# Stick-breaking attention: carrying the sum over later key tiles inside the softplus terms instead of by matmuls of its own

## The chip, the cores and the metric

The kernel runs on one core of a Trainium2 chip. The metric is the device time of one execution in microseconds (us). One execution was also taken by the hardware profiler; its trace says when each instruction of each engine ran.

## What is computed

One layer of a decoder trunk: 512 tokens of width 1024. The layer has a mixer (stick-breaking attention beside a gated convolution), a cross-attention into 256 memory tokens and a gated feed-forward part. The change lies in the stick-breaking attention, 8 heads of width 64:

```python
z = jnp.einsum('bhqd,bhkd->bhqk', qb, kb) * scale
...
mask = k_pos < q_pos
log_fail = jnp.where(mask, jax.nn.log_sigmoid(-z), 0.0)
log_later = lax.cumsum(log_fail, axis=3, reverse=True) - log_fail
weights = jnp.where(mask, jnp.exp(jax.nn.log_sigmoid(z) + log_later), 0.0)
outs.append(jnp.einsum('bhqk,bhkd->bhqd', weights, vb))
```

With softplus(z) = -log_sigmoid(-z), the exponent of a weight is z minus the sum of softplus(z) over its own key and all later keys up to the query.

## The kernel before

All products are made in three passes of fp32r matmuls: each operand is split into a high part (a cast on ScalarE) and a low part (a subtraction on VectorE). The layer starts with the projection of values (to about 28 us), then comes the attention stage, then merging, memory attention, the feed-forward part and the output. TensorE's order in the attention stage is written out by hand (`manual_schedule`). ScalarE, VectorE, GpSimd and the DMA queue of SyncE are ordered there by a scheduler, from priorities, and each of them runs its instructions in that order.

The stage is a list of 16 steps, `steps`: head pair p = 0 to 3, and for each the key tiles kt = 3, 2, 1, 0 of 128 keys, the latest first. Scores are kept with keys on the 128 partitions and queries along the row; a tile kt has n = 512 - 128 kt queries. At kt=3 and kt=2 both heads of a pair share one PSUM bank (`z`, 2n columns), at kt=1 and kt=0 each head has its own. A step has three parts, which three functions emit.

- `scores` makes z = k q (L388 for kt=3 and 2, L395 on 64 partitions for kt=1 and 0), then the softplus e of z: three activations of ScalarE (L402 to L404), one operation of VectorE (L405), the causal mask on GpSimd (L355), and the split of e into the parts l (`lsplit`: L375 on ScalarE, L376 on VectorE). It also copies row 0 of z (L412, L417).
- `weights` adds to z, in PSUM, minus the running sum of softplus: `negtri` is a triangle of -1, and L438 multiplies it with the two parts of l. What the later tiles bring is added by matmuls of its own: L428 at kt=2, L434 once for each head at kt=1 and kt=0. They multiply a matrix `ones`, which holds -1 in four rows and 0 elsewhere, with the tile `rows` (named carry in the trace), which holds the carried sum of each head in a high and a low row. For the tile after, the new carried sum is row 0 of z as it was minus row 0 as it is now (L443, L448); a cast (L455) and a subtraction (L456) split it. Then come exp (L451), the mask, and the split of the weights a into ah and al (L462, L463).
- `values` multiplies the weights with v (L474), and after kt=0 the pair's output is added up and split (L482, L483, L169, L170).

TensorE's order around step i is: some halves of projections, which fill the time (L155 to L157, `fill_some`), `scores` of step i+1, `weights` of step i, `values` of step i-1. The halves bring q and k of the next pair, the convolution's inputs and some gates. Their weights are loaded by SyncE (`wr`, 512 KB each), cast (`wh`, L150) and subtracted (`wl`, L151). SyncE also moves the second half of the queries into `lq` (L300) and loads the memory tokens `mk` (L490). The latter are squared on ScalarE (L497) and summed on GpSimd (L500, L502).

Of the kernel before, what the change touches and what calls it, by code (L numbers as in the profile page):

```python
# [26 lines left out]
HS = S // 2  # L27
# [13 lines left out]
def hybrid_layer(ctx: ExitStack, tc: tile.TileContext, xT_d, memT_d, cols_d, wv_d, win_d,  # L41
                 wbr_d, wmix_d, wmq_d, wmk_d, wmv_d, wmo_d, wfi_d, wfo_d, out):
    nc = tc.nc
# [10 lines left out]
    lpool = stick.enter_context(tc.tile_pool(name="lpool", bufs=4))  # L54
# [153 lines left out]
    first = nc.scalar.dma_start(gcol, cols_d)  # L208
# [130 lines left out]

    oT = []  # L340
    steps = [(p, kt) for p in range(TT) for kt in range(TT - 1, -1, -1)]
    zs, sp, av, ops = {}, {}, {}, {}

    def span(kt):
        return kt * P, S - kt * P

    def by_head(t, kt):

        n = span(kt)[1]
        if 2 * n <= 512:  # L350
            return [t[0].rearrange("p (h n) -> p h n", n=n)]
        return [u[:, None, :] for u in t]

    def causal(t):
        nc.gpsimd.affine_select(out=t[:, :, :P], in_=t[:, :, :P], compare_op=ALU.is_gt, fill=0.0,  # L355
                                base=0, pattern=[[0, t.shape[1]], [1, P]], channel_multiplier=-1)

    rows = [lpool.tile([P, n], F32R, tag=f"carry{n}", name=f"carry{n}", bufs=1) for n in (S, HS)]  # L360
    raw_rows = [lpool.tile([P, S], F32, tag=f"row{i}", name=f"row{i}", bufs=1) for i in range(2)]
    for t in rows:
        nc.gpsimd.memset(f(t), 0.0)
    ones_f = tmp("ones", P)
    nc.gpsimd.memset(ones_f, 0.0)
    for i in range(0, P, HD // 2):
        nc.gpsimd.memset(ones_f[i:i + 1, :], -1.0)
    ones = lpool.tile([P, P], F32R, tag="ones", name="ones", bufs=1)
    nc.vector.tensor_copy(ones, ones_f)
    first = {}  # L370

    def lsplit(t, n, tag):
        hi, lo = (lpool.tile([P, n], F32R, tag=tag, name=nm(tag), bufs=4,
                             padded_shape=[P, S if tag == "l0" else S - P]) for _ in range(2))
        nc.scalar.copy(hi, t)  # L375
        nc.vector.tensor_tensor(out=lo, in0=t, in1=f(hi), op=ALU.subtract)  # L376
        return hi, lo

    def scores(p, kt):
        c0, n = span(kt)  # L380
        q, k = qk[p]
        ks = slice(kt * P, (kt + 1) * P)
        terms = (0, 0), (0, 1), (1, 0)
        if 2 * n <= 512:
            zs[p, kt] = [ztile("z")[:, :2 * n]]
            z3 = by_head(zs[p, kt], kt)[0]
            for i, (a, b) in enumerate(terms):
                nc.tensor.matmul(z3, k[a][:, ks], late_q[p % 2][b][:, :, c0 - HS:],  # L388
                                 start=i == 0, stop=i == 2)
        else:  # L390
            zs[p, kt] = [ztile("z")[:, :n] for _ in range(2)]
            for i, (a, b) in enumerate(terms):
                for h in range(2):
                    hs = slice(h * HD, (h + 1) * HD)
                    nc.tensor.matmul(zs[p, kt][h], k[a][hs, ks], q[b][hs, c0:],  # L395
                                     start=i == 0, stop=i == 2)
        sp[p, kt] = []
        with tc.high_priority(100):
            for h, z in enumerate(zs[p, kt]):
                w = z.shape[1]  # L400
                e = tmp("e")[:, :w]
                nc.scalar.activation(e, z, AF.Abs)  # L402
                nc.scalar.activation(e, e, AF.Exp, scale=-1.0)
                nc.scalar.activation(e, e, AF.Ln, bias=1.0)  # L404
                nc.vector.scalar_tensor_tensor(out=e, in0=z, scalar=0.0, in1=e, op0=ALU.max,  # L405
                                               op1=ALU.add)
                causal(by_head([e], kt)[0])
                sp[p, kt].append(lsplit(e, w, f"l{kt % 2}"))

                if kt == TT - 1:  # L410
                    first[p, kt] = [raw_rows[kt % 2][0:1, :w]]
                    nc.scalar.copy(first[p, kt][0], z[0:1, :])  # L412
                elif kt > 0:
                    for i in range(2) if w == 2 * n else (h,):
                        r = raw_rows[kt % 2][i * HD:i * HD + 1, :n]
                        first.setdefault((p, kt), []).append(r)
                        nc.scalar.copy(r, head_of(p, kt, i)[0:1, :])  # L417

    def head_of(p, kt, h):
        n = span(kt)[1]  # L420
        z = zs[p, kt]
        return z[0][:, h * n:(h + 1) * n] if len(z) == 1 else z[h]

    def weights(p, kt):
        c0, n = span(kt)
        av[p, kt] = []
        if kt == TT - 2:
            nc.tensor.matmul(by_head(zs[p, kt], kt)[0][:, :, P:], ones,  # L428
                             rows[1].rearrange("p (h n) -> p h n", h=2), start=False, stop=False,
                             skip_group_check=True)  # L430
        elif kt < TT - 2:
            for h in range(2):
                hs = slice(h * HD, (h + 1) * HD)
                nc.tensor.matmul(zs[p, kt][h][:, P:], ones[hs, :], rows[0][hs, :n - P],  # L434
                                 start=False, stop=False, skip_group_check=True)
        for z, parts in zip(zs[p, kt], sp[p, kt]):
            for part in parts:
                nc.tensor.matmul(z, negtri, part, start=False, stop=True, skip_group_check=True)  # L438
        exp_a = []
        got = first.get((p, kt), [])  # L440
        with tc.high_priority(150):
            if kt == TT - 1:
                nc.vector.tensor_tensor(out=got[0], in0=got[0], in1=zs[p, kt][0][0:1, :],  # L443
                                        op=ALU.subtract)
            for h, z in enumerate(zs[p, kt]):
                if 0 < kt < TT - 1:
                    for i in range(2) if len(zs[p, kt]) == 1 else (h,):
                        nc.vector.tensor_tensor(out=got[i], in0=got[i],  # L448
                                                in1=head_of(p, kt, i)[0:1, :], op=ALU.subtract)
                exp_a.append(tmp("a")[:, :z.shape[1]])  # L450
                exps.append(nc.scalar.activation(exp_a[h], z, AF.Exp))  # L451
            for h, r in enumerate(got):
                i = h * HD
                c = rows[1 if kt == TT - 1 else 0][:, :r.shape[1]]
                nc.scalar.copy(c[i:i + 1, :], r)  # L455
                nc.vector.tensor_tensor(out=c[i + HD // 2:i + HD // 2 + 1, :], in0=r,  # L456
                                        in1=f(c[i:i + 1, :]), op=ALU.subtract)
        for a in exp_a:
            causal(by_head([a], kt)[0])
            w = a.shape[1]  # L460
            ah, al = unit("ah")[:, :w], unit("al")[:, :w]
            nc.vector.tensor_copy(ah, a)  # L462
            nc.vector.tensor_tensor(out=al, in0=a, in1=f(ah), op=ALU.subtract)  # L463
            for i in range(w // n):
                av[p, kt].append((ah[:, i * n:(i + 1) * n], al[:, i * n:(i + 1) * n]))
# [490 lines left out]
    hs = HS  # L956
# [147 lines left out]
```

## Time and profile before

| | us |
|---|---|
| median of 3 runs (864.08 to 864.14) | 864.14 |
| the profiled execution | 864.6 |
| its span, first to last instruction | 861.8 |

| stretch of the span | TensorE busy | VectorE busy | ScalarE busy |
|---|---|---|---|
| 28 to 49 us | 21.00 of 21 | 13.83 | 11.47 |
| 49 to 202 us (16 steps of attention) | 152.66 of 153 | 132.12 | 110.11 |
| 202 to 862 us | 654.00 of 660 | 416.56 | 299.57 |

The engines are called PE (TensorE matmuls), PEld (its loads of weights), DVE (VectorE), ACT (ScalarE), POOL (GpSimd) and SP (SyncE) in the rows. In a timeline's row stand the start, the duration, the engine, the line, the operation, the tiles written and read, and their shapes; in brackets the idle time before it and what ended it. Matmuls overlap, and their ends are modelled: how long one holds TensorE is read from its start to the start of the next. In a row of a group stand the count, the busy time, the mean of one in ns, and the idle time before.

### The profile page before, as it was taken

How to read it: one execution, taken by the hardware profiler on the slowest of the kernel's cores; microseconds unless marked ns; L12 is line 12 of the kernel's file. 1: busy time of each engine (PE TensorE's matmuls, PEld its weight loads, DVE VectorE, ACT ScalarE, POOL GpSimd, SP SyncE). 2: the span in 40 equal slices, each digit the busy share in tenths (PEclk: the TensorE clock that was granted, in tenths of full speed). 3: DMA queues.
4: the chain of work that ended last, by engine and by line, in shares of the span. 5: the costliest groups of instructions: out<-in, count | busy, mean ns of one | idle time of the engine just before them, and what ended most of it. 6: DMA issues, size and time to landing. Idle time of an engine off the chain costs nothing.

```text
span 861.8 us, 12717 instructions
## 1 busy us (share of the span) xinstructions
PE 854.1 (99%) x4932; PEld 750.9 (87%) x4932; DVE 586.9 (68%) x964; ACT 440.2 (51%) x774; POOL 69.2 (8%) x105
## 2 busy tenths in 40 slices
PE   9999999999999999999999999999999999999997
PEld 7887888888888898888888889999999999888897
DVE  8768898986555466555555879888887778533334
ACT  7476787675333244443444656555445556322335
POOL 2022131111000000000000101111111100000002
PEclk9999999999999999999999999999999999999999
DMA  8432331228333345422111427777677763322202
GB/s 294 131 101 86 106 115 50 74 84 266 115 110 110 98 159 188 154 97 93 57 49 49 135 50 199 188 182 178 175 190 192 188 151 122 123 98 98 74 1 97
DMA packets 42347, 108.32 MB, mean 126 GB/s; under 512 B 4144, under 2 KB 8240, under 8 KB 42288
## 3 DMA queue, kind: packets, MB, share of 16 engines
q1 hardware_dynamic: 36016, 95.70, 32.8%
q0 software_dynamic: 5984, 11.54, 8.2%
q8 instruction: 38, 0.62, 0.3%
q10 hardware_dynamic: 288, 0.29, 0.1%
q14 instruction: 21, 0.17, 0.1%
HBM read 104.36 MB, written 2.10 MB: 124 GB/s over the span
## 4 chain that ended last, share of the span: by engine, by line
PE 98%; DVE 1%; ACT 0%; issue 0%; POOL 0%; DVEq 0%; POOLq 0%
PE z L811 15%; PE y L811 7%; PE pr L155 7%; PE pr L157 7%; PE pr L156 7%; PE f L157 5%; PE f L155 5%; PE f L156 5%; PE v L811 4%; PE r L155 3%; PE r L156 3%; PE r L157 3%; PE v L261 3%; PE mq L155 2%; PE mq L157 2%; PE mq L156 2%
## 5 line engine op out<-in xcount | busy, mean ns | idle before, releaser
L150 ACT CAST wh<-wr 128x1024 fp32r<-128x1024 f32 x106 | 111.0, 1051 | 215.2 <-issue 98.6
L151 DVE TENSOR_TENSOR wl<-wr,wh 128x1024 fp32r<-128x1024 f32 x106 | 129.4, 1223 | 100.0 <-ACT wh L150 100.0
L155 PE MATMUL pr<-xgh,wh 128*128 128x512 f32 x288 | 112.5, 391 | 0.0
L156 PE MATMUL pr<-xgl,wh 128*128 128x512 f32 x288 | 112.2, 390 | 0.0
L157 PE MATMUL pr<-xgh,wl 128*128 128x512 f32 x288 | 112.2, 390 | 0.0
L156 PE MATMUL f<-actl,wh 128*128 128x512 f32 (+1 forms) x208 | 74.2, 357 | 0.0
L155 PE MATMUL f<-acth,wh 128*128 128x512 f32 (+1 forms) x208 | 74.2, 357 | 0.0
L157 PE MATMUL f<-acth,wl 128*128 128x512 f32 (+1 forms) x208 | 74.0, 356 | 0.0
L811 PE MATMUL z<-xdh,wf 128*128 128x256 f32 x352 | 70.3, 283 | 0.0
L768 POOL DMA_DIRECT2D ws<-in_w_ffn_in_dram x22 | 26.6, 1208 | 468.7 <-DVE c L626 267.3
L157 PEld LDWEIGHTS pr<-xgh,wl 128*128 128x128 f32 x288 | 54.1, 188 | 11.4
L156 PEld LDWEIGHTS pr<-xgl,wh 128*128 128x128 f32 x288 | 54.1, 188 | 10.8
L155 PEld LDWEIGHTS pr<-xgh,wh 128*128 128x128 f32 x288 | 54.1, 188 | 10.8
L811 PEld LDWEIGHTS z<-xdh,wf 128*128 128x128 f32 x352 | 58.0, 192 | 0.0
L831 ACT COPY sa<-z 128x256 f32<-128x256 f32 x44 | 16.4, 373 | 77.8 <-PE z L811 77.8
L811 PE MATMUL z<-xdl,wf 128*128 128x256 f32 x176 | 49.8, 283 | 0.0
L802 DVE TENSOR_TENSOR wf<-s,wf 128x512 fp32r<-128x512 f32 x44 | 30.3, 690 | 20.9 <-ACT wf L801 19.8
L155 PEld LDWEIGHTS f<-acth,wh 128*128 128x128 f32 x208 | 39.3, 189 | 5.7
L157 PEld LDWEIGHTS f<-acth,wl 128*128 128x128 f32 x208 | 39.3, 189 | 5.6
L156 PEld LDWEIGHTS f<-actl,wh 128*128 128x128 f32 x208 | 39.3, 189 | 5.6
L811 PE MATMUL y<-xch,wf 128*128 128x256 f32 x176 | 35.5, 283 | 0.0
L811 PE MATMUL v<-xoh,wf 128*128 128x256 f32 x176 | 35.5, 283 | 0.0
(290 smaller groups left out, 2158.9 us busy)
## 6 DMA issues: line engine op xcount, KB each, us to landing
wr<-in_w_in_dram SPq DMA_DIRECT2D x36, 512.0 KB, 3.3
ws<-in_w_ffn_in_dram SPq DMA_DIRECT2D x22, 512.0 KB, 3.8
wg<-in_w_ffn_in_dram SPq DMA_DIRECT2D x22, 512.0 KB, 4.2
ws<-in_w_ffn_in_dram POOLq DMA_DIRECT2D x22, 512.0 KB, 5.7
wr<-in_w_ffn_out_dram SPq DMA_DIRECT2D x22, 512.0 KB, 3.2
a<-in_w_ffn_in_dram SPq DMA_DIRECT2D x22, 256.0 KB, 4.6
wr<-in_w_branch_dram SPq DMA_DIRECT2D x8, 512.0 KB, 3.2
wr<-in_w_mem_k_dram SPq DMA_DIRECT2D x8, 512.0 KB, 3.2
```

The costliest lines, as they stand in the source:

```text
L150: after(nc.scalar.copy(h2, raw), lead[-1:])
L151: lows.append(nc.vector.tensor_tensor(out=l2, in0=raw, in1=f(h2), op=ALU.subtract))
L155: nc.tensor.matmul(ps, a[0], b[0], start=start, stop=False, **kw)
L156: nc.tensor.matmul(ps, a[0], b[1], start=False, stop=False, **kw)
L157: nc.tensor.matmul(ps, a[1], b[0], start=False, stop=stop, **kw)
L261: nc.tensor.matmul(vps[t], xg[k][a][:, sl], wv[k][b], start=k == 0 and (a, b) == (0, 0), stop=k == KD - 1 and a == 1)
L768: nc.gpsimd.dma_start(s13, a[:, 0:4:3, :], accum_op=ALU.add)
L802: nc.vector.tensor_tensor(out=lo, in0=raw, in1=f(hi), op=ALU.subtract)
L811: nc.tensor.matmul(ps[:, :HS], a, b, start=i < 3 and k == 0 and j == 0, stop=k == KP - 1 and j == 2, skip_group_check=True)
L831: nc.scalar.copy((s[:, :HS], None, None, s[:, HS:], t[:, :HS])[i], z)
```

## The change

The carried sum is no longer multiplied in. It is added to the last row (partition 127) of the softplus tile e of the next key tile, before e is split into high and low parts; the triangle in L438 then brings it to all keys of the tile. To do so:

- `scores` ends with e, and the split moves into a new function `parts`, which the loop calls for step i+1 after `weights` of step i.
- Row 0 of z is copied straight into partition 0 of a tile `carries`, and the subtraction is made there in place. A DMA on SyncE's queue takes the result to partition 127 of the same tile.
- `parts` adds partitions 96 to 127 of `carries` (of which only 127 is not zero) to e.
- The matrix `ones`, the matmuls L428 and L434, and the cast and subtraction of the carried row go.

```diff
-    rows = [lpool.tile([P, n], F32R, tag=f"carry{n}", name=f"carry{n}", bufs=1) for n in (S, HS)]
-    raw_rows = [lpool.tile([P, S], F32, tag=f"row{i}", name=f"row{i}", bufs=1) for i in range(2)]
...
+    carries = [lpool.tile([P, n], F32, tag=f"carry{n}", name=f"carry{n}", bufs=1)
+               for n in (S, S + HS)]
+    for t in carries:
+        nc.gpsimd.memset(t, 0.0)
...
                 causal(by_head([e], kt)[0])
+                es[p, kt].append(e)
+                if kt > 0:
+                    r = carries[kt % 2][0:1, h * w:(h + 1) * w]
+                    first.setdefault((p, kt), []).append(r)
+                    nc.scalar.copy(r, z[0:1, :])
+
+    def parts(p, kt):
+        c0, n = span(kt)
+        sp[p, kt] = []
+        with tc.high_priority(100):
+            for h, e in enumerate(es.pop((p, kt))):
+                w = e.shape[1]
+                if kt < TT - 1:
+                    c = carries[(kt + 1) % 2][P - 32:P, h * w // n * (n - P):]
+                    c = c[:, :w // n * (n - P)].rearrange("p (h n) -> p h n", n=n - P)
+                    e3 = e.rearrange("p (h n) -> p h n", n=n)[P - 32:P, :, P:]
+                    nc.vector.tensor_tensor(out=e3, in0=e3, in1=c, op=ALU.add)
                 sp[p, kt].append(lsplit(e, w, f"l{kt % 2}"))
...
     def weights(p, kt):
...
-        if kt == TT - 2:
-            nc.tensor.matmul(by_head(zs[p, kt], kt)[0][:, :, P:], ones,
-                             rows[1].rearrange("p (h n) -> p h n", h=2), start=False, stop=False,
-                             skip_group_check=True)
-        elif kt < TT - 2:
-            for h in range(2):
-                hs = slice(h * HD, (h + 1) * HD)
-                nc.tensor.matmul(zs[p, kt][h][:, P:], ones[hs, :], rows[0][hs, :n - P],
-                                 start=False, stop=False, skip_group_check=True)
...
+            for r, z in zip(got, zs[p, kt]):
+                nc.vector.tensor_tensor(out=r, in0=r, in1=z[0:1, :], op=ALU.subtract)
...
             for h, r in enumerate(got):
-                i = h * HD
-                c = rows[1 if kt == TT - 1 else 0][:, :r.shape[1]]
-                nc.scalar.copy(c[i:i + 1, :], r)
-                nc.vector.tensor_tensor(out=c[i + HD // 2:i + HD // 2 + 1, :], in0=r,
-                                        in1=f(c[i:i + 1, :]), op=ALU.subtract)
+                w = r.shape[1]
+                nc.sync.dma_start(carries[kt % 2][P - 1:P, h * w:(h + 1) * w], r)
...
     scores(*steps[0])
+    parts(*steps[0])
...
                 weights(*steps[i])
             else:
                 gate(EARLY, 0)
+            if i + 1 < len(steps):
+                parts(*steps[i + 1])
             if i > 0:
                 values(*steps[i - 1])
```

Two places where the built order moved, besides those that the prediction shows. On TensorE, around `weights` of step 1, before:

```order
L395 MATMUL z_637<-qkh_444,qkl_486 128x384
L428 MATMUL z_566<-carry_397,ones 128x2x128
L438 MATMUL z_566<-l_576,negtri 128x512
L438 MATMUL z_566<-l_577,negtri 128x512
L474 MATMUL o_682<-ah_590,v_382 128x128
```

L428 and the other 19 matmuls of `ones` are taken out, and TensorE's order is otherwise the same. On SyncE, around the rows of step 2, in the changed kernel:

```order
L444 DMA carry_396<-carry_396 1x16x32
L143 DMA wr_1206<-in_w_in_dram 128x1024
L143 DMA wr_1284<-in_w_in_dram 128x1024
L444 DMA carry_397<-carry_397 1x16x24 x2
L477 DMA mk_783<-in_memT_dram 128x2x256
```

The rows of a step (one DMA at kt=3 and kt=2, two at kt=1) stand between the loads of weights.

More of the change, by code (lines that the diff above doesn't have):

```diff
@@ L341, in hybrid_layer @@
     steps = [(p, kt) for p in range(TT) for kt in range(TT - 1, -1, -1)]
-    zs, sp, av, ops = {}, {}, {}, {}
+    zs, es, sp, av, ops = {}, {}, {}, {}, {}
     def span(kt):
@@ L356, in causal @@
                                 base=0, pattern=[[0, t.shape[1]], [1, P]], channel_multiplier=-1)
-    rows = [lpool.tile([P, n], F32R, tag=f"carry{n}", name=f"carry{n}", bufs=1) for n in (S, HS)]
-    raw_rows = [lpool.tile([P, S], F32, tag=f"row{i}", name=f"row{i}", bufs=1) for i in range(2)]
[L362 to L369, printed above, removed]
+    carries = [lpool.tile([P, n], F32, tag=f"carry{n}", name=f"carry{n}", bufs=1)
+               for n in (S, S + HS)]
+    for t in carries:
+        nc.gpsimd.memset(t, 0.0)
     first = {}
@@ L396, in scores @@
                                      start=i == 0, stop=i == 2)
-        sp[p, kt] = []
+        es[p, kt] = []
         with tc.high_priority(100):
@@ L407, in scores @@
                 causal(by_head([e], kt)[0])
-                sp[p, kt].append(lsplit(e, w, f"l{kt % 2}"))
[L410 to L417, printed above, removed]
+                es[p, kt].append(e)
[14 more added lines that the diff above has]
+                    nc.vector.tensor_tensor(out=e3, in0=e3, in1=c, op=ALU.add)
+                sp[p, kt].append(lsplit(e, w, f"l{kt % 2}"))
     def head_of(p, kt, h):
@@ L426, in weights @@
         av[p, kt] = []
-        if kt == TT - 2:
-            nc.tensor.matmul(by_head(zs[p, kt], kt)[0][:, :, P:], ones,
-                             rows[1].rearrange("p (h n) -> p h n", h=2), start=False, stop=False,
-                             skip_group_check=True)
-        elif kt < TT - 2:
-            for h in range(2):
-                hs = slice(h * HD, (h + 1) * HD)
-                nc.tensor.matmul(zs[p, kt][h][:, P:], ones[hs, :], rows[0][hs, :n - P],
-                                 start=False, stop=False, skip_group_check=True)
-        for z, parts in zip(zs[p, kt], sp[p, kt]):
-            for part in parts:
+        for z, both in zip(zs[p, kt], sp[p, kt]):
+            for part in both:
                 nc.tensor.matmul(z, negtri, part, start=False, stop=True, skip_group_check=True)
@@ L441, in weights @@
         with tc.high_priority(150):
-            if kt == TT - 1:
-                nc.vector.tensor_tensor(out=got[0], in0=got[0], in1=zs[p, kt][0][0:1, :],
-                                        op=ALU.subtract)
+            for r, z in zip(got, zs[p, kt]):
+                nc.vector.tensor_tensor(out=r, in0=r, in1=z[0:1, :], op=ALU.subtract)
             for h, z in enumerate(zs[p, kt]):
[L446 to L449, printed above, removed]
                 exp_a.append(tmp("a")[:, :z.shape[1]])
```

## The prediction

> **What bounds the kernel now.** I read the page first, then the stage in which the change lies (the table of stretches, 49 to 202 us), then the waits of TensorE there.
>
> ```profile
> PE 854.1 (99%) x4932; PEld 750.9 (87%) x4932; DVE 586.9 (68%) x964; ACT 440.2 (51%) x774; POOL 69.2 (8%) x105
> PE 98%; DVE 1%; ACT 0%; issue 0%; POOL 0%; DVEq 0%; POOLq 0%
> 49.00:202.00 153.00, 152.66 (x722) 123.44 (x722) 132.12 (x226) 110.11 (x209) 30.17 (x57) 1.00 0.29 96
> PE z L438 <- DVE l L376: 0.3, 1, 0.3
> ```
>
> TensorE is the chain: 98% of it over the whole span. In the attention stage it is busy 152.66 of 153.00 us at full granted clock, and it waited for another engine once, 0.3 us. So time taken from TensorE there is time of the kernel, as long as nothing else becomes late. What could become late is VectorE (132.12 of 153, 86%) and, behind it, ScalarE (110.11, 72%). The stage has 16 steps: four head pairs p, and in each the key tiles kt = 3, 2, 1, 0. I call them 0 to 15; step 5 is p=1, kt=2.
>
> **What goes from TensorE.** Twenty matmuls: L428 once a pair (kt=2), L434 twice at kt=1 and at kt=0. The timeline of TensorE shows what they take, from start to start (ends are modelled):
>
> ```profile
> 75.97 0.28 PE L388 MATMUL z<-lq,qkl 128*128 128x256 f32 x1
> 76.18 0.44 PE L434 MATMUL z<-carry,ones 64*128 64x384 f32 x2
> 76.55 0.96 PE L438 MATMUL z<-l,negtri 128*128 128x512 f32 x3
> 77.83 0.50 PE L438 MATMUL z<-l,negtri 128*128 128x512 f32 x1 [0.31 <-DVE l L376]
> 78.16 0.33 PE L474 MATMUL o<-ah,v 128*128 128x384 f32 x1
> 78.33 0.34 PE L474 MATMUL o<-al,v 128*128 128x384 f32 x1
> ```
> ```profile
> 92.19 0.34 PE L395 MATMUL z<-qkh,qkl 64*128 64x384 f32 x2
> 92.46 0.38 PE L428 MATMUL z<-carry,ones 128*128 128x256 f32 x1
> 92.68 0.63 PE L438 MATMUL z<-l,negtri 128*128 128x512 f32 x2
> ```
> ```profile
> 102.43 0.40 PE L395 MATMUL z<-qkh,qkl 64*128 64x512 f32 x2
> 102.66 0.29 PE L434 MATMUL z<-carry,ones 64*128 64x256 f32 x2
> 102.88 0.97 PE L438 MATMUL z<-l,negtri 128*128 128x384 f32 x4
> 103.69 0.28 PE L474 MATMUL o<-ah,v 128*128 128x256 f32 x1
> 103.80 0.28 PE L474 MATMUL o<-al,v 128*128 128x256 f32 x1
> ```
>
> In a stream, 256 columns take 0.11 us (103.69 to 103.80) and 384 take 0.17 (78.16 to 78.33). A pair on 64 rows each runs side by side. So at kt=0 the pair L434 should take 0.17; it takes 0.37 (76.18 to 76.55), and the 256-column L388 ahead of it takes 0.21 instead of 0.11. Two gaps of 0.1 to 0.2 stand where the row shape goes from 128 to 64 and back. Without the pair no shape changes there, so 0.37 + 0.10 = about 0.45 goes. At kt=2, L428 takes 0.22 (92.46 to 92.68), and the gap of 0.10 ahead of it (0.27 instead of 0.17) stays, since L395 is on 64 rows and L438 on 128: 0.22 goes. At kt=1, L434 is on 64 rows like L395; of its 0.22 the change of shape (0.11) stays for L438: 0.11 goes. A pair: 0.45 + 0.22 + 0.11 = 0.78, four pairs 3.1 us. Columns alone would be 0.17 + 0.11 + 0.11 = 0.39, 1.6 us in all: the lower bound. I take 3.1, since the gaps stand in the starts.
>
> The Trainium skill says under "Tiling Modes" of TensorEngine Tiling (Array Packing) that changing the tiling mode drains TensorE; the gaps of 0.10 to 0.20 agree. By that rule the sum is the 3.1; without it, the 1.6.
>
> The wait at 77.83 also costs: the fourth L438 of that step would start at 76.55 + 3 x 0.23 = 77.24, so 0.6 us is lost there now. Upper bound of the gain: 3.1 + 0.6 = 3.7.
>
> **What changes on VectorE and ScalarE.** The groups by form, in the stage:
>
> ```profile
> L456 DVE TENSOR_TENSOR carry<-row,carry 1x256 fp32r<-1x256 f32 x12 | 5.2, 431 | 3.5 <-ACT carry L455 3.2
> L456 DVE TENSOR_TENSOR carry<-row,carry 1x384 fp32r<-1x384 f32 x8 | 4.5, 566 | 0.3
> L455 ACT CAST carry<-row 1x256 fp32r<-1x256 f32 x12 | 4.7, 396 | 0.8 <-DVE row L448 0.7
> L455 ACT CAST carry<-row 1x384 fp32r<-1x384 f32 x8 | 4.1, 506 | 5.6 <-DVE row L448 5.5
> ```
>
> ScalarE loses the 20 casts (4.7 + 4.1 = 8.8 us) and the 6.2 us for which it stood waiting in front of them. VectorE loses the 20 low parts (9.7 us) and 3.2 us of waits for those casts. It gains 20 adds of the carried row into the softplus tile, on 32 partitions. No row shows one; a one-partition and a full operation of 256 columns take the same (L443 and L463 below, 0.40 and 0.41), so I take 0.4 for 256 columns and 0.55 for 384: 12 x 0.4 + 8 x 0.55 = 9.2. VectorE's own work is even; it loses waits.
>
> The new part is the way of the row: after L443 or L448 (the subtraction, now in place), a DMA of one row from partition 0 to 127, then the add, then the cast and the low part, then L438. Before, the matmul took it, and the split of the softplus terms waited for nothing of the step before. The order of VectorE at step 5, first before:
>
> ```order
> L443 TENSOR_TENSOR row_399<-row_399,z_861 1x256
> L456 TENSOR_TENSOR carry_397<-row_399,carry_397 1x256
> L462 COPY ah_965<-a_960 128x256
> L405 TENSOR_SCALAR e_945<-z_941,e_945 128x512
> L463 TENSOR_TENSOR al_966<-a_960,ah_965 128x256
> L483 TENSOR_TENSOR ot_973<-o_682,ot_973 64x512
> L483 TENSOR_TENSOR ot_973<-o_683,ot_973 64x512
> L376 TENSOR_TENSOR l_952<-e_945,l_951 128x512
> L294 TENSOR_SCALAR qk_999<-pr_928,r0b_338 128x512
> ```
>
> and in the changed kernel (L438 is the subtraction there, L420 the add, L370 the low part l):
>
> ```order
> L438 TENSOR_TENSOR carry_397<-carry_397,z_845 1x256
> L449 COPY ah_941<-a_937 128x256
> L399 TENSOR_SCALAR e_927<-z_923,e_927 128x512
> L450 TENSOR_TENSOR al_942<-a_937,ah_941 128x256
> L470 TENSOR_TENSOR ot_954<-o_668,ot_954 64x512
> L420 TENSOR_TENSOR e_927<-e_927,carry_397 32x2x128
> L470 TENSOR_TENSOR ot_954<-o_669,ot_954 64x512
> L294 TENSOR_SCALAR qk_980<-pr_910,r0b_338 128x512
> L370 TENSOR_TENSOR l_947<-e_927,l_946 128x512
> ```
>
> The add stands four operations behind the subtraction, and an output operation, the eviction qk and l stand behind it: if the row has not landed, all three wait. The DMA stands in SyncE's queue at this place, in the changed kernel:
>
> ```order
> L300 DMA lq_388<-qkh_896 64x256 x2
> L143 DMA wr_1443<-in_w_in_dram 128x1024
> L444 DMA carry_397<-carry_397 1x16x16
> L300 DMA lq_389<-qkl_897 64x256 x2
> L477 DMA mk_963<-in_memT_dram 128x2x256
> ```
>
> It stands right behind a 512 KB load of weights, in the slot that the second pair of lq had. What such a slot costs is seen in the trace (median us to landing, then SyncE's timeline):
>
> ```profile
> lq<-qkh SPq DMA_DIRECT2D x8, 64.0 KB, 2.0
> lq<-qkl SPq DMA_DIRECT2D x8, 64.0 KB, 3.6
> ```
> ```profile
> 86.74 0.53 SPq L143 DMA_DIRECT2D wr<-in_w_in_dram  x1
> 87.32 1.10 SPq L300 DMA_DIRECT2D lq<-qkl  x2
> ```
> ```profile
> 86.52 0.40 DVE L443 TENSOR_TENSOR row<-row,z 1x256 f32<-1x256 f32 x1
> 87.66 0.43 DVE L456 TENSOR_TENSOR carry<-row,carry 1x256 fp32r<-1x256 f32 x1 [0.73 <-ACT carry L455]
> 88.93 0.41 DVE L463 TENSOR_TENSOR al<-a,ah 128x256 fp32r<-128x256 f32 x1
> 89.26 1.40 DVE L483 TENSOR_TENSOR ot<-o,ot 64x512 f32<-64x512 f32 x2
> 90.69 0.69 DVE L376 TENSOR_TENSOR l<-e,l 128x512 fp32r<-128x512 f32 x1
> ```
>
> The walk of step 5, by the clock of before: the row is ready at 86.92 and issued at 87.32. It lands at 89.3 (2.0 us) or 90.9 (3.6). Then the add 0.4, output 0.7, qk 0.7, l 0.7 = 2.5: l is there at 91.8 or 93.4. TensorE wants it for its second L438 of the step, at 92.68 + 0.23 = 92.9, less what it has won by then (0.78 + 0.22 and part of the 0.6, about 1.2): at 91.7. So 0.1 or 1.7 us of stall. But VectorE should be earlier by then. ScalarE's order at step 3 moves the square of a memory tile (mk, L497 before, L484 now) ahead of the last cast of l; before:
>
> ```order
> L150 COPY wh_1092<-wr_1090 128x1024
> L375 COPY l_755<-e_749 128x512
> L375 COPY l_765<-e_759 128x512
> L169 COPY yh_838<-gb_835 128x512
> L402 ACTIVATE e_865<-z_861 128x256
> L497 ACTIVATE mk_799<-mk_799 128x512
> L451 ACTIVATE a_882<-z_741 128x512
> ```
>
> and now:
>
> ```order
> L150 COPY wh_1070<-wr_1068 128x1024
> L369 COPY l_770<-e_735 128x512
> L484 ACTIVATE mk_783<-mk_783 128x512
> L369 COPY l_775<-e_741 128x512
> L396 ACTIVATE e_849<-z_845 128x256
> L169 COPY yh_822<-gb_819 128x512
> L441 ACTIVATE a_860<-z_727 128x512
> ```
>
> It moved up three places. Before, GpSimd's sum waited for it, the mask of a behind that sum, and VectorE for the mask:
>
> ```profile
> 78.00 0.62 ACT L497 ACTIVATE mk<-mk 128x512 f32<-128x512 f32 x1
> 78.70 2.22 POOL L502 TENSOR_TENSOR accm<-accm,mk 128x256 f32<-128x256 f32 x2 [3.18 <-ACT mk L497]
> 81.20 0.49 DVE L462 CAST ah<-a 128x512 fp32r<-128x512 f32 x1 [1.70 <-POOL a L355]
> ```
>
> With mk some 2 to 3 us earlier the 1.70 us of VectorE's wait goes, and the subtraction of step 4, in order behind it, can come up to 1.7 earlier. That covers the 3.6 landing at step 5 but for rests. At kt=1 and kt=0 there are 10 us and more between one step's L438 and the next (92.68, 102.88), so a landing of 3.6 is hidden; at step 13 this bounds it:
>
> ```profile
> 168.01 0.69 DVE L376 TENSOR_TENSOR l<-e,l 128x512 fp32r<-128x512 f32 x1
> 170.44 0.63 PE L438 MATMUL z<-l,negtri 128*128 128x512 f32 x2
> ```
>
> l ended at 168.7 and is wanted at 170.7: 2.0 us of slack for a lead of up to 3. I take 0.2 of stall at each of steps 5, 9 and 13, 0.6 in all, and half of the 0.6 at step 3 as won. If VectorE's cover is gone, the price is rival 1.
>
> **Sum.** 3.1 + 0.3 - 0.6 = 2.8 us. The profiled execution took 864.6 us (861.8 of span, 2.8 around it), so 861.8 by its own time; the median of the runs is 864.14, so 861.3. Of 864.14, 0.2% (about what a measurement can tell) is 1.7 us. The likeliest case alone spans 860.4 (gain 3.7) to 862.4.
>
> **Rivals.** 1: VectorE does not come earlier, and the rows land after 3.6. Then step 5 is late by 93.4 - 92.9 = 0.5 against before, and the lead starts anew: kt=1 and kt=0 of p=1, then p=2 and p=3, 0.56 + 2 x 0.78 = 2.1, less 0.5: gain 1.6, 862.5, within 0.2%. For it: VectorE is at 86%; against it: the waits that go. Chance 0.12.
>
> 2: the mode gaps stay and only columns go: 1.6 + 0.3 - 0.6 = 1.3, 862.8. Against it: the starts above. Chance 0.08.
>
> 3, slower: a one-row DMA of 64-byte pieces behind a weight load lands much later than the 64 KB ones. At p=1 and p=2 each us beyond 3.6 stops TensorE for one us at kt=2, since l waits. Zero gain is at 3.6 + 1.6/2 = 4.4; at 5.5 it is 2 x 1.9 - 1.6 = 2.2 slower, 866.3. For it: the 2.0 against 3.6 above, and most of the rows follow a weight load; against it: only one row moves. Chance 0.20.
>
> The Trainium skill, "Queues, rings and completion order" of DMA: Bandwidth & Descriptors, says that a DMA's semaphore increment lands only after every earlier write of that DMA engine. By that rule a carried row cannot count as landed before the weights ahead of it; the trace agrees (3.6 against 2.0), and it speaks for rivals 1 and 3.
>
> That the matmuls do not go is excluded by the order: TensorE has 20 rows fewer and no other difference. Loads of weights are not held up by rows: each stands behind an operation of VectorE that comes later than the subtraction anyway.
>
> **Numbers.** Forecast 0.60, rivals 0.12, 0.08 and 0.20. Faster by over 0.2%: 0.60; within: 0.20; slower: 0.20. The range goes from 860.4 (gain 3.7) to 864.8 (rival 3 with a landing of 4.7: 0.7 slower), which leaves out the rest of rival 3.
>
> **What would show it.** Right: no L428 and L434; L388 to L438 in 0.11 to 0.13 us at kt=0; stage shorter by about 3 us; TensorE's waits for l under 1 us in all; the ah after step 3 without its 1.70. Wrong: waits of TensorE for l of a us or more at kt=2, with VectorE's add waiting for the DMA just before; rows of the carry with a median landing over 4 us.

## The result and the profile after

The changed kernel takes 862.63 us (median of 21 runs, 861.09 to 863.11), the kernel before 863.73 in the same comparison: 1.1 us less, ratio 0.9986 with a 95% interval of 0.9979 to 0.9992. In a second comparison on another occasion (e11 below) it was 861.82 against 863.77, 1.95 us less, ratio 0.9978 (0.9968 to 0.9987). So the kernel is faster, by 0.13 to 0.23%: about at the 0.2% (1.7 us) that the prediction set as a bound, and less than the 2.8 us of the forecast.

The page's first lines, the stretch of the attention stage in the table of stretches, and the waits of TensorE in it, answering to those of before:

```profile
PE 851.6 (99%) x4912; PEld 749.1 (87%) x4912; DVE 587.1 (68%) x959; ACT 431.3 (50%) x750; POOL 69.7 (8%) x100
PE 96%; DVE 2%; DMA 0%; issue 0%; POOL 0%; DVEq 0%; SPq 0%; ACT 0%; POOLq 0%
```
```profile
49.00:202.00 153.00, 150.85 (x707) 122.25 (x706) 132.60 (x223) 102.19 (x187) 31.26 (x57) 1.00 0.31 97
```
```profile
PE z L433 <- DVE l L370: 2.1, 2, 1.5
```

TensorE has its 20 matmuls less. In the stage it is now busy 150.85 us of 153 in place of 152.66, and what it is not busy it waits for l: 2.1 us in 2 waits, where it was 0.3 in one. A part of what the matmuls gave back has become waiting. (L433 is the triangle's matmul that was L438, L382 and L389 the scores, L370 the low part of l, L438 now the subtraction, L420 the add of the carried row, L444 its DMA.)

TensorE's timeline at the three places that the prediction priced, at the stage's first L433 (49.55), and at the two places where it waits (56.45 and 57.49 are step 1, 77.26 and 79.81 step 3):

```profile
49.55 0.76 PE L433 MATMUL z<-l,negtri 128*128 128x256 f32 x2
...
56.45 0.49 PE L433 MATMUL z<-l,negtri 128*128 128x512 f32 x1
57.49 0.50 PE L433 MATMUL z<-l,negtri 128*128 128x512 f32 x1 [0.54 <-DVE l L370]
...
77.14 0.28 PE L382 MATMUL z<-lq,qkl 128*128 128x256 f32 x1
77.26 1.02 PE L433 MATMUL z<-l,negtri 128*128 128x512 f32 x3
79.81 0.50 PE L433 MATMUL z<-l,negtri 128*128 128x512 f32 x1 [1.53 <-DVE l L370]
...
94.20 0.34 PE L389 MATMUL z<-qkh,qkl 64*128 64x384 f32 x2
94.47 0.73 PE L433 MATMUL z<-l,negtri 128*128 128x512 f32 x2
...
104.33 0.40 PE L389 MATMUL z<-qkh,qkl 64*128 64x512 f32 x2
104.65 0.97 PE L433 MATMUL z<-l,negtri 128*128 128x384 f32 x4
```

From the last scores matmul to the first L433 it is now 0.12 us at kt=0 (0.58 before), 0.27 at kt=2 (0.49) and 0.32 at kt=1 (0.45): 0.46 + 0.22 + 0.13 = 0.81 a pair, 3.2 us in four. Against it stand two losses, both in the first head pair. In step 1 the second L433 would start at 56.45 + 0.23 = 56.68 and starts at 57.49: 0.8 lost, where nothing was lost before. In step 3 the fourth would start at 77.26 + 3 x 0.23 = 77.95 and starts at 79.81: 1.86 lost, where it was 0.6. So 3.2 - 0.8 - 1.26 = 1.1 us is left.

Step 1 is a row that lands late. VectorE's timeline there, SP's timeline, and the DMAs issued from 46 to 56 us (KB, us to landing):

```profile
55.16 0.42 DVE L420 TENSOR_TENSOR e<-e,carry 32x256 f32<-32x256 f32 x1 [1.34 <-DMA carry<-carry]
55.61 1.23 DVE L151 TENSOR_TENSOR wl<-wr,wh 128x1024 fp32r<-128x1024 f32 x1
56.75 0.68 DVE L370 TENSOR_TENSOR l<-e,l 128x512 fp32r<-128x512 f32 x1
```
```profile
49.21 0.54 SPq L143 DMA_DIRECT2D wr<-in_w_in_dram  x1
...
51.09 0.56 SPq L444 DMA_DIRECT2D carry<-carry  x1
```
```profile
wr<-in_w_in_dram SPq DMA_DIRECT2D x1, 512.0 KB, 3.9
...
carry<-carry SPq DMA_DIRECT2D x1, 1.0 KB, 4.0
```

The row is issued 1.9 us behind a 512 KB load of weights and lands 4.0 us later. The add waits 1.34 us for it, and 1.23 us of weights (wl) stand between it and l. In the kernel before, the l of this step began at 54.52, behind the same wl, with no row to wait for.

Step 3 is another thing: the row is there, but two of VectorE's operations take nearly twice as long while GpSimd sums the memory's squares. VectorE's timeline, then GpSimd's:

```profile
76.20 0.69 DVE L334 TENSOR_TENSOR gb<-pr,r0b 128x512 f32<-128x512 f32 x1
76.81 0.68 DVE L370 TENSOR_TENSOR l<-e,l 128x512 fp32r<-128x512 f32 x1
77.40 1.23 DVE L335 TENSOR_TENSOR gb<-gb,cv 128x512 f32<-128x512 f32 x1
78.56 1.21 DVE L370 TENSOR_TENSOR l<-e,l 128x512 fp32r<-128x512 f32 x1
...
81.52 0.51 DVE L449 CAST ah<-a 128x512 fp32r<-128x512 f32 x1
```
```profile
76.92 2.29 POOL L489 TENSOR_TENSOR accm<-accm,mk 128x256 f32<-128x256 f32 x2 [1.17 <-ACT mk L484]
```

The same operation on the same shape takes 0.68 at 76.81 and 1.21 at 78.56. Before, that sum ran at 78.70, behind the last l. VectorE's timeline before:

```profile
77.08 0.69 DVE L376 TENSOR_TENSOR l<-e,l 128x512 fp32r<-128x512 f32 x1
...
78.82 0.68 DVE L170 TENSOR_TENSOR yl<-gb,yh 128x512 fp32r<-128x512 f32 x1
```

Here l took 0.69, and so did the gb ahead of it (76.48). The sum stood beside yl there, and it was GpSimd that lost: the first of its two additions took 1.40 us, where one with VectorE idle beside it for most of its time takes 0.73 (56.22), and yl took 0.68. Which of the two engines has to wait thus differs from case to case; what decides it no run here shows. The ah that waited 1.70 us for the mask waits no more (81.52 has no bracket), as forecast; the sum that made room for it now lies on top of l.

### The profile page after: what moved, and what is told of

It reads as the page before. It is cut to its first block, busy times and chain, and to the rows that moved or that the text cites. A ratio compares the mean times of both kernels' runs of the same rounds, so it can differ in the third digit from the quotient of the medians.

```text
span 861.1 us, 12693 instructions
## 1 busy us (share of the span) xinstructions
PE 851.6 (99%) x4912; PEld 749.1 (87%) x4912; DVE 587.1 (68%) x959; ACT 431.3 (50%) x750; POOL 69.7 (8%) x100
## 4 chain that ended last, share of the span: by engine, by line
PE 96%; DVE 2%; DMA 0%; issue 0%; POOL 0%; DVEq 0%; SPq 0%; ACT 0%; POOLq 0%
PE z L801 15%; PE y L801 7%; PE pr L155 7%; PE pr L156 7%; PE pr L157 7%; PE f L157 5%; PE f L155 5%; PE f L156 5%; PE v L801 4%; PE r L156 3%; PE r L157 3%; PE r L155 3%; PE v L261 3%; PE mq L157 2%; PE mq L156 2%; PE mq L155 2%
## 5 line engine op out<-in xcount | busy, mean ns | idle before, releaser
L801 PE MATMUL z<-xdl,wf 128*128 128x256 f32 x176 | 49.8, 283 | 0.0
```

The costliest lines, as they stand in the source:

```text
L801: nc.tensor.matmul(ps[:, :HS], a, b, start=i < 3 and k == 0 and j == 0, stop=k == KP - 1 and j == 2, skip_group_check=True)
```

## Experiments

Theory A: TensorE's saving is the full 3.2 us, and two things in pair 0 take back 2 us: the late row of step 1, and GpSimd's sum in step 3. Its rivals: only the streamed columns go (1.6 us), or VectorE has too much to do there, so that any wait taken away comes back elsewhere. All times are medians; each is set against the kernel before in the same comparison.

**e1, TensorE's saving alone.** In the kernel before:

```diff
-        if kt == TT - 2:
-            nc.tensor.matmul(by_head(zs[p, kt], kt)[0][:, :, P:], ones, ...
-        elif kt < TT - 2:
-            for h in range(2):
-                nc.tensor.matmul(zs[p, kt][h][:, P:], ones[hs, :], rows[0][hs, :n - P], ...
```

> The kernel before with its 20 carry matmuls (L428 and L434) taken out and everything else kept: the rows are still subtracted, rounded and written, only nobody adds them to z, so the sum over later key tiles is left out of z. It measures TensorE's saving alone, without the change's row transfers, adds and new order. Theory A (the forecast's first term: columns and mode gaps both go, 0.45 + 0.22 + 0.11 a pair, four pairs) expects about 3.1 us less than the kernel before, near 860.6, and the wait for l at step 3 still there (0.3 to 0.9 us lost). The rival (the gaps stay where the tiling changes, only the streamed columns go) expects 1.6 us less, near 862.1. If TensorE is held by l in this stage whatever is taken from it, under 1 us less.

Measured: 860.66 against 863.89, 3.2 us less, ratio 0.9967 (0.9956 to 0.9979). TensorE's timeline (L429 is the triangle's matmul here, L388 and L395 the scores):

```profile
75.49 0.28 PE L388 MATMUL z<-lq,qkl 128*128 128x256 f32 x1
75.60 0.40 PE L429 MATMUL z<-l,negtri 128*128 128x512 f32 x1
76.36 0.73 PE L429 MATMUL z<-l,negtri 128*128 128x512 f32 x2 [0.35 <-DVE l L376]
77.56 0.50 PE L429 MATMUL z<-l,negtri 128*128 128x512 f32 x1 [0.47 <-DVE l L376]
...
91.93 0.34 PE L395 MATMUL z<-qkh,qkl 64*128 64x384 f32 x2
92.20 0.73 PE L429 MATMUL z<-l,negtri 128*128 128x512 f32 x2
```

0.11 us and 0.27, as in the changed kernel. Step 3 lost 77.56 - (75.60 + 0.69) = 1.27 us, more than the 0.3 to 0.9 expected: TensorE is there 0.95 us sooner than before (75.60 against 76.55), the last l only 0.25 (76.83 against 77.08). So 0.7 us comes back as waiting, as the last rival has it, and the trace leaves 3.2 - 0.7 = 2.5 us; that too lies within the interval. The columns alone would be 1.6 us, outside the interval (1.8 to 3.8 us). The gaps of the tiling change are real time, and they went.

**e2, GpSimd's sum taken out of step 3.**

```diff
-        for j in range(2):
+        for j in range(2 if k2 != 1 else 0):
             if k2 + j == 0:
```

> The changed kernel without one pair of additions on GpSimd: the second memory tile's squares are not added to accm (the pair that runs in step 3 at 76.92); the square itself stays, and no other instruction changes its place on any engine. Theory A (in step 3 GpSimd's sum runs beside VectorE's gb L335 and l L370 and stretches them from 0.69 to 1.22 us each) expects those two at 0.69 us, the fourth L433 about 1.07 us earlier against the third (stall 1.53 becomes about 0.5), and the whole kernel about 1.1 us shorter, near 861.6. The rival (the second half of l is late because ScalarE's square of mk stands ahead of its cast, or because VectorE simply has too much to do) expects the stall to stay at 1.3 to 1.5 us and the time at 862.6.

Measured: 861.14 against 863.89, 2.75 us less, ratio 0.9971 (0.9960 to 0.9981). VectorE's timeline, then TensorE's:

```profile
77.43 0.69 DVE L335 TENSOR_TENSOR gb<-gb,cv 128x512 f32<-128x512 f32 x1
78.04 0.68 DVE L370 TENSOR_TENSOR l<-e,l 128x512 fp32r<-128x512 f32 x1
```
```profile
77.29 1.02 PE L433 MATMUL z<-l,negtri 128*128 128x512 f32 x3
78.78 0.51 PE L433 MATMUL z<-l,negtri 128*128 128x512 f32 x1 [0.47 <-DVE l L370]
```

Both operations are back at 0.69, and the fourth matmul starts 1.49 us after the first of the group in place of 2.55. ScalarE's square still stands ahead of the cast of l here, so it is not what made l late.

**e3, the row's wait taken out of step 1.**

```diff
                     c = carries[(kt + 1) % 2][P - 32:P, h * w // n * (n - P):]
+                    if (p, kt) == (0, 2):
+                        c = zero[P - 32:P, :]
```

> The changed kernel, where the one add of step 1 (pair 0, kt = 2) reads a tile of zeros in place of the carried row, so it waits for no transfer; the row's DMA is still issued, and the carried sum is left out of that one key tile. The add comes one place earlier on VectorE (ahead of the product qk), nothing else moves. Theory A (step 1's loss is the row landing 4.0 us after its issue, behind a weight load) expects the 1.34 us wait of VectorE gone, the stall of TensorE before the second group of L433 in step 1 (0.54 us, 0.8 us lost) gone, step 3's stall of about 1.5 us unchanged, and 0.8 us less in all, near 861.8. The rival (VectorE has too much work in pair 0, and a wait taken away at one place comes back at the next) expects 862.6.

Measured: 861.79, 2.1 us less than before, ratio 0.9978 (0.9969 to 0.9987). TensorE's timeline (L437 is the triangle's matmul here and in e4):

```profile
56.19 0.73 PE L437 MATMUL z<-l,negtri 128*128 128x512 f32 x2
...
78.77 0.50 PE L437 MATMUL z<-l,negtri 128*128 128x512 f32 x1 [1.55 <-DVE l L372]
```

The two matmuls of step 1 run on without a stall, and step 3's stall is untouched.

**e4, both**, with the sum moved to step 4 in place of taken out:

```diff
-MEM_AT = (1, 3, 5, 7)
+MEM_AT = (1, 4, 5, 7)
...
+                    if (p, kt) == (0, 2):
+                        c = zero[P - 32:P, :]
```

> The changed kernel with e3's edit, and with the second memory tile's load, square and sum moved from step 3 to step 4 (MEM_AT = (1, 4, 5, 7)), so that GpSimd's sum does not run beside step 3's l; the carried sum is left out of one key tile of pair 0 as in e3. Theory A expects the two gains to add: 0.8 + 1.1 us less than the changed kernel, near 860.7, about 3.0 us under the kernel before, which is the forecast's TensorE saving (3.1) with only the old wait at step 3 left (0.6 to 0.8 us lost); no new stall at steps 4 and 5. The rival (one of the two makes up for the other, or the moved sum holds VectorE up in step 4 instead) expects 861.5 to 862.0, with a stall for l in step 4 or 5.

Measured: 860.59, 3.3 us less than before, ratio 0.9965 (0.9952 to 0.9977). The waits of TensorE in the stage:

```profile
PE z L437 <- DVE l L372: 0.5, 1, 0.5
```

One wait is left, that of step 3 which the kernel before had too. Each of the two edits takes away its own stall and leaves the other's (e2, e3), so the gains add: 3.0 us by the trace, 3.3 measured (2.0 to 4.1).

**e5 and e8, the sum moved alone, in the changed kernel and in the kernel before.** The first line of e4's diff, and nothing else.

> The changed kernel, whole, with only the second memory tile's load, square and sum moved from step 3 to step 4 (MEM_AT = (1, 4, 5, 7)). Theory A (GpSimd's sum beside gb and l costs 1.0 to 1.1 us in step 3, and nothing of the kind waits in step 4) expects step 3's stall at about 0.5 us as without the sum, no stall in step 4, step 1's stall of about 0.5 us unchanged, and 861.5, some 2.2 us under the kernel before. The rival (the sum costs the same wherever it stands) expects 862.5 with a new stall for l in step 4 or 5.

> The kernel before, whole, with the second memory tile's load, square and sum moved from step 3 to step 4 in the same way. It tells whether e5's gain belongs to the change or to the move. Theory A (in the kernel before the sum runs after the last l of step 3, so it costs TensorE nothing) expects no difference from the kernel before: 863.8, within 0.3 us, with the wait for l at step 3 as it is. The rival (the sum costs about 1 us there too) expects 862.7.

Measured: e5 860.98 against 863.41, 2.4 us less, ratio 0.9970 (0.9959 to 0.9981). e8 863.68, ratio 1.0000 (0.9992 to 1.0009): in the kernel before the sum's place is worth nothing. It is the change that made it costly, by bringing it in front of l. In e5 GpSimd's sum stands here:

```profile
84.53 1.88 POOL L489 TENSOR_TENSOR accm<-accm,mk 128x256 f32<-128x256 f32 x2 [3.37 <-ACT mk L484]
```

and no wait of TensorE appears in step 4 or 5. Step 1 lost only 0.26 us in this profile (the group of two took 0.99 us where it takes 0.73), since the row landed in 3.4 us, not in 4.0.

**e6 and e7, the late row on another queue**, both on top of e5:

```diff
-                nc.sync.dma_start(carries[kt % 2][P - 1:P, h * w:(h + 1) * w], r)
+                queue = nc.gpsimd if (p, kt) == (0, TT - 1) else nc.sync    # e7: nc.scalar
+                queue.dma_start(carries[kt % 2][P - 1:P, h * w:(h + 1) * w], r)
```

> e5 with one more edit: the first row of pair 0 (kt = 3) is sent by GpSimd's DMA queue in place of SP's; no other instruction moves. Theory A (that row took 4.0 us because on SP's queue it stood behind a 512 KB weight load and a 64 KB copy) expects it to land in 2.0 to 2.7 us, VectorE's 1.34 us wait to shrink to under 0.2 us, step 1's stall to go, and about 0.8 us less than e5, near 860.7. The rival (the row is late because the 16 DMA engines themselves are full then, whichever queue asks, or because this queue is slow to begin) expects a landing of 4 us or more and e5's time, 861.5, or up to 0.5 us above it.

> e5 with the first row of pair 0 sent by ScalarE's DMA queue, issued behind its exp of a. In step 1 two pairs of VectorE's instructions change places: al comes ahead of e, and the low part of qk ahead of that of l (0.6 us later for l). Theory A expects the row to land in 2.0 to 2.7 us, l about 0.7 us earlier than in e5 (1.34 less wait, 0.6 more work ahead), a stall of 0 to 0.2 us in step 1, and 860.7 to 860.9. The rival (DMA engines full) expects a landing of 4 us and, with l moved back, a stall of about 1.1 us in step 1 and 862.0.

Measured: e6 861.35, ratio 0.9973 (0.9962 to 0.9984); e7 861.46, ratio 0.9974 (0.9964 to 0.9984): 2.0 us under the kernel before, no better than e5. The DMA groups of e6, then of e7:

```profile
carry<-carry POOLq DMA_DIRECT2D x1, 1.0 KB, 3.8
```
```profile
carry<-carry ACTq DMA_DIRECT2D x1, 1.0 KB, 4.0
```

Here my theory, that the row stands in SP's queue, fell: the row is as late from any queue. The times say less than the landings: in e6 GpSimd issues the row (0.72 us) ahead of the mask of a, and VectorE waited 1.85 us for that mask in place of 1.00; in e7 l then came behind the low part of qk too, and TensorE waited 1.16 us in step 1.

**e9 and e10, which transfer holds it up.** Theory B: the 512 KB load of weights, in the DMA engines that all queues share. In e9 that load is issued behind the row:

```diff
         i = nc.sync.dma_start(raw, src)
+        loads.append(i)
+        if len(loads) == 11:
+            after(i, row_dma[:1])
```

and in e10 the load stays ahead of the row, and the copies of lq beside it are cut short:

```diff
-                nc.sync.dma_start(f(t)[hs, h, :], f(u)[hs, HS:])
+                part = 8 if p == 1 else HS
+                nc.sync.dma_start(f(t)[hs, h, :part], f(u)[hs, HS:HS + part])
```

> e5, whole, with one more edit: the 512 KB weight load that SP issues some 2 us ahead of the first row of pair 0 is issued right behind that row (its weights are cast only some 23 us later). No other instruction changes its place. e6 and e7 showed that another queue does not help (3.8 and 4.0 us). Theory B (the row stands behind the weight load in the DMA engines themselves, whichever queue issues it) expects the row to land in 1.6 to 2.4 us, VectorE's wait for it gone, no stall in step 1, and 0.3 to 0.8 us less than e5, 860.3 to 860.7. The rival (it is the 64 KB copies of qkl, or the 256 KB load that follows it, that hold it up) expects a landing of 3.4 to 4.0 us as before and e5's time, 861.0.

> e5 with the four copies of lq for pair 1 cut from 256 columns to 8 (2 KB in place of 64 KB each), two of which SP issues just ahead of and just behind the first row of pair 0; scores of pair 1's late queries are left out by it. It is looked at for the landing of that row alone. Theory B (the weight load holds it up) expects 3 us or more still. The rival (the copies hold it up) expects 2.4 us or less.

The DMA groups from 46 to 56 us, of e9 and then of e10:

```profile
wr<-in_w_in_dram SPq DMA_DIRECT2D x1, 512.0 KB, 3.5
...
carry<-carry SPq DMA_DIRECT2D x1, 1.0 KB, 1.7
```
```profile
lq<-qkh SPq DMA_DIRECT2D x2, 2.0 KB, 1.7
lq<-qkl SPq DMA_DIRECT2D x2, 2.0 KB, 3.5
carry<-carry SPq DMA_DIRECT2D x1, 1.0 KB, 3.5
```

With the load behind it the row lands in 1.7 us. With the load ahead and the copies short it still takes 3.5; and copies of 2 KB take 1.7 ahead of the load and 3.5 behind it. So the load makes the difference. The 512 KB load that e9 issues 0.6 us behind the row does not delay it. (e10 ran once, at 861.26 us, and its time says nothing.)

But a load ahead is not enough. The next row of the changed kernel (2 KB, issued at 58.73) also stands 1.87 us behind a 512 KB load. The DMA group of 56 to 60 us:

```profile
carry<-carry SPq DMA_DIRECT2D x1, 2.0 KB, 1.6
```

It landed at 60.3, 0.3 us behind its load; the row of step 1 landed at 55.1, 2.0 us behind its load (49.21 + 3.9 = 53.1). Copies of lq stand beside the row of step 1 and not beside the other. By themselves they do no harm (e9), and their bytes do not matter (e10). What makes these 2 us out of load and copies is open.

e9 took 860.63 against 863.77, 3.1 us less, ratio 0.9967 (0.9955 to 0.9980); the second group of step 1 lost 0.04 us (e5: 0.26). Its interval overlaps e5's: by time the two can't be told apart. It computes all that the kernel before computes, and has the lowest median among the kernels here of which that is true.

VectorE still waited 0.57 us for that row in e9, since it was issued at 52.77 (50.67 in e5): both copies of qkl stand ahead of it here, where one did in e5, and they took 1.90 us to issue in place of 1.10. Why is open.

**e11, the changed kernel again.**

> The changed kernel unaltered, beside e9 on the same chip: a second profile of it. Expected: 0.9 to 1.4 us under the kernel before; the stalls again at the second group of step 1 (0.3 to 0.6 us) and the fourth matmul of step 3 (1.5 us), both the same within 0.3 us; the start of the stage (first L433 at 49.55 in the first profile) anywhere from 48.8 to 49.8, since it has differed by that much among profiles of kernels that are alike up to there. If the late start belongs to the change it will be at 49.5 again.

Measured: 861.82, 1.95 us less than before. TensorE's timeline:

```profile
49.20 0.76 PE L433 MATMUL z<-l,negtri 128*128 128x256 f32 x2
56.10 0.49 PE L433 MATMUL z<-l,negtri 128*128 128x512 f32 x1
57.05 0.50 PE L433 MATMUL z<-l,negtri 128*128 128x512 f32 x1 [0.46 <-DVE l L370]
...
79.39 0.50 PE L433 MATMUL z<-l,negtri 128*128 128x512 f32 x1 [1.53 <-DVE l L370]
```

Both stalls are there again, and the stage began at 49.20. In the profiles here it begins anywhere from 48.8 (e1) to 49.8 (e8, e9), in both kernels and their variants alike; the 0.5 us by which the first profile of the changed kernel started late is not the change's.

**e12, what of GpSimd's work holds VectorE up.** The sum's two additions became four writes, as long together:

```diff
+        if k2 == 1:
+            for _ in range(4):
+                nc.gpsimd.memset(mk, 0.0)
-        for j in range(2):
+        for j in range(2 if k2 != 1 else 0):
```

> The changed kernel, where the two additions of GpSimd in step 3 are replaced by four writes of zeros to the same memory tile (0.52 us each by the profile's rows, 2.1 us together, in place of 2.29), at the same place and behind the same square; the second memory tile is so left out of the sum, and no other instruction moves. It tells what of GpSimd's work holds VectorE up. Theory A1 (two engines that both read two operands from SBUF get in each other's way; writes alone do not) expects gb L335 and l L370 at 0.69 us as without the sum, step 3's stall at 0.5 us, and 861.0 to 861.6. The rival A2 (any GpSimd work on SBUF at that time slows VectorE) expects 1.0 to 1.2 us for each, the stall at 1.0 to 1.5 us, and 861.8 to 862.6.

Measured: 861.30 against 863.97, 2.7 us less, ratio 0.9968 (0.9955 to 0.9980). GpSimd's timeline, then VectorE's:

```profile
76.21 2.28 POOL L487 MEMSET mk<- 128x512 f32 x4 [1.15 <-ACT mk L484]
```
```profile
76.71 0.68 DVE L335 TENSOR_TENSOR gb<-gb,cv 128x512 f32<-128x512 f32 x1
77.31 0.69 DVE L370 TENSOR_TENSOR l<-e,l 128x512 fp32r<-128x512 f32 x1
```

GpSimd is as busy as with the sum (2.28 us against 2.29), beside the same two operations, and they take 0.68 and 0.69. Here writes cost VectorE nothing, and an addition that reads two tiles from SBUF does.

The Trainium skill, SBUF — State Buffer, "Who interferes with whom", says just this: a VectorE instruction with two SBUF inputs contends with a GpSimd instruction that reads SBUF, and not with one that only writes. The rows agree in both halves: 1.23 and 1.21 us beside the sum, 0.68 and 0.69 beside the writes. It also calls the shared port an exclusive lock; the l at 76.81 in the changed kernel, which began 0.11 us ahead of the sum, took its usual 0.68.

Put together, with the stalls read from each trace as above (3.2 us, less step 1's loss, less what step 3 loses beyond the old 0.6):

| kernel | lost in step 1 | lost in step 3 | left by the trace | measured |
|---|---|---|---|---|
| changed | 0.81 | 1.86 | 1.1 | 1.1 |
| e11 | 0.72 | 1.86 | 1.2 | 1.95 |
| e2 | 0.80 | 0.80 | 2.2 | 2.75 |
| e3 | 0 | 1.88 | 1.9 | 2.1 |
| e4 | 0 | 0.80 | 3.0 | 3.3 |
| e5 | 0.26 | 0.79 | 2.75 | 2.4 |
| e6 | 0.91 | 0.80 | 2.1 | 2.1 |
| e7 | 1.42 | 0.80 | 1.6 | 1.95 |
| e9 | 0.04 | 0.97 | 2.8 | 3.1 |
| e12 | 0.31 | 0.79 | 2.7 | 2.7 |

The intervals of the measured column are 0.6 to 1.1 us to either side, so single rows prove little; the order of the rows, and the traces, carry it.

## Why the prediction was half right

**The matmuls: right in sum.** Forecast 0.78 a pair (0.45, 0.22, 0.11) and 3.1 us; the starts give 0.81 (0.46, 0.22, 0.13) and 3.2, and e1 measured 3.2 (1.8 to 3.8). Rival 2, columns only, is refuted. On this the Trainium skill's rule of a drain at a change of tiling mode (TensorEngine Tiling (Array Packing), "Tiling Modes") was the right side to stand on: the gaps went with the shape changes at kt=0, and stayed at kt=2, where 0.27 us still lie ahead of L433.

The forecast is right for the sum only. Read one matmul further, from the last scores to the first values matmul, the parts are others: 0.56 at kt=0 (1.61 us before, 1.05 now, at step 7, which has no stall), 0.13 at kt=2 (0.96, 0.83) and 0.13 at kt=1 (1.26, 1.13), 0.82 a pair. With L428 gone the two L433 at kt=2 take 0.09 us longer, and at kt=0 the four take 0.10 less. So the term of kt=2 was too large, that of kt=0 too small, and that they balance is luck.

**Step 3: the step that failed.** The prediction took "half of the 0.6 at step 3 as won", 0.3 us. Instead 1.26 us more were lost there, a miss of 1.6 us, nearly the whole difference between 2.8 and 1.1 (in e11, with 1.95, the forecast was missed by 0.9). Of the 1.26, 1.06 is GpSimd's sum (e2); the other 0.2 I did not trace. TensorE wins 0.46 us just ahead of the wait, which comes back as waiting when l does not come sooner; in e1 0.7 did. The prediction gave no row for an earlier l there: the 1.70 us wait that was to go stands at 81.20, behind the last l of step 3 (77.08), and could not bring it forward. It had seen the cause, and quoted it: ScalarE's square of mk moves ahead of the last cast of l, so GpSimd's sum comes earlier. It followed that only to who waits for the sum (the mask, then ah: the 1.70 us did go), and not to what then runs at the same time as it. An operation that is moved ahead of another engine's critical work must be priced for running beside it.

**Late rows: the size was about right, the place wrong.** Forecast were 0.2 us at each of steps 5, 9 and 13, 0.6 in all; lost were 0.8, all in step 1, which the walk left out. The rows took 1.6 to 4.0 us, and the cover of VectorE's earlier subtraction held at step 5, by VectorE's timeline:

```profile
91.12 0.42 DVE L420 TENSOR_TENSOR e<-e,carry 32x256 f32<-32x256 f32 x1
```

No wait stands before the add; the row landed in 3.1 us, as the DMA group of 84 to 96 us has it:

```profile
carry<-carry SPq DMA_DIRECT2D x1, 1.0 KB, 3.1
```

In step 1 the row took 4.0 us, and wl stands between the add and l, which it does not in step 5.

**Rivals.** Rival 1 (862.5) and the measured time are close, but not by its mechanism: VectorE did come earlier (its subtraction of step 4 began 0.44 us behind TensorE's L433, 87.47 - 87.03, in place of 1.49, 86.52 - 85.03), and no lead had to start anew at p=1. Rival 3 needed landings over 4.4 us; the longest is 4.0. (By its own formula a landing of 4.7 is 2 x 1.1 - 1.6 = 0.6 us slower, not the 0.7 of the range; nothing hangs on it.) In the changed kernel eight of the twelve steps that send rows issued them 0.4 to 1.1 us behind a 512 KB load; these rows took 2.6 to 3.4 us and landed 0.15 to 0.25 us behind that load. The Trainium skill's rule that a DMA's semaphore lands only after every earlier write of its DMA engine (DMA: Bandwidth & Descriptors, "Queues, rings and completion order") agrees with these rows, and with 1.7 against 3.5 to 4.0 us. The page says that it holds across queues, which e6 and e7 bear out and my first theory of step 1 had overlooked. The 2.0 us by which the row of step 1 landed behind its load do not follow from it.

**The signs named.** 0.11 to 0.13 us at kt=0: 0.12. The ah without its wait: so. Waits for l under 1 us in all: no, 2.1. The stage shorter by about 3 us: no; the span is 0.7 shorter, and 1.2 without the 0.5 of the later start. The sign of being wrong, an add that waits for its DMA ahead of a stall at kt=2, came once, in step 1.

## What to carry to other kernels

When work leaves the bounding engine, price the new order of the others too: look for what a moved instruction will run beside, not only for who waits for it. Before a small transfer is put on a short path, look for large loads issued just ahead of it, on any queue; move the load, not the transfer. Here the two repairs, a few lines, bring the kernel from 861.82 us (861.21 to 863.11, 10 runs) to 860.63 (860.01 to 861.38, 5 runs) in one comparison.

## What the runs showed of the hardware

GpSimd's sum of two SBUF tiles and VectorE's operations on two SBUF tiles hold each other up: 0.69 us became 1.21 to 1.23, two such operations lost 1.07 us, and the two additions took 2.29 us together. In the kernel before GpSimd lost in their place: 1.40 us for an addition of 0.73, while yl took 0.68. GpSimd's writes of the same length cost VectorE nothing. A row of 1 KB from one partition to another lands in 1.7 us with no load just ahead (e9). Issued 0.4 to 1.1 us behind a 512 KB load, rows landed 0.15 to 0.25 us behind that load, 2.6 to 3.4 us after their issue. The row of step 1, 1.6 to 2.2 us behind its load and with copies of lq beside it, took 3.4 to 4.0 us, from SP's, ScalarE's and GpSimd's queue alike; a row 1.87 us behind a load without such copies took 1.6.
